# Four column groups of an input projection by seven products, in a stage of their own

## The chip, the cores and the metric

The kernel runs on 1 core of one Trainium2 chip. The metric is the device time of one execution in microseconds (us), lower is better. The kernel before takes 2202.64 us, the median of 3 runs (2201.62 to 2202.83).

## The reference, cut to what matters

One transformer block for 512 tokens of width 2048, in float32. Its first matrix product, `h @ w_in`, is 6680 columns wide and feeds two kinds of attention; then come the output projection, two norms and an MLP of width 8192.

```python
h = rms_norm(x, norm_mix_pre)
proj = h @ w_in                                   # [512, 2048] @ [2048, 6680]
q_a, kv_a, gate_a, q_r, k_r, v_r, g_r = split(proj)   # 1024, 1536, 24, 4 x 1024
kv6 = kv_a.reshape(S, 6, 2, 128)                  # six kinds, two groups of heads, 128 wide
k_cmp = compress_kv(kv6[:, 0], ...)               # gelu(blocks of 32 rows @ w1 + b1) @ w2
v_cmp = compress_kv(kv6[:, 1], ...)
o_a = nsa_attention(q_a, k_cmp, v_cmp, kv6[:, 2], kv6[:, 3], kv6[:, 4], kv6[:, 5],
                    sigmoid(gate_a), t5_bias)     # compressed + selected + window, gated sum
o_r = silu(g_r) * retention(rope(q_r), rope(k_r), v_r)   # four heads of 256
x = x + rms_norm(concat(o_a, o_r) @ w_out, norm_mix_post)
u = square(relu(rms_norm(x, norm_mlp_pre) @ w_up))
x = x + rms_norm(u @ w_down, norm_mlp_post)
```

## The kernel before, in words

**Products in three terms.** Every large product splits both operands into a high and a low part (`split`, L141: ScalarE casts the high part, VectorE subtracts it for the low part). `mm3` (L153) issues three matmuls per tile: high x high, high x low, low x high. The normed input lies in SBUF, transposed, as `Hh` and `Hl` (16 tiles of 128 features by 512 tokens each).

**Slabs and blocks.** A `Slab` (L168) is two feature tiles (256 rows) of up to 512 columns of a weight matrix: `fetch` starts its DMA on SP's queue into a ring of three raw buffers (`wr`), `load` splits it into one of three pairs `whi`, `wlo` (pool `wp`). A block of a projection is eight slabs. `feat_major` (L202) yields outputs with features on the partitions: the weights are the stationary operand, 512 tokens move. `tok_major` (L224) yields outputs with tokens on the partitions: the tokens are stationary and the columns move. One step of the block's work is a chunk of six matmuls; a slab has four chunks. `Driver.run` (L273) walks through the slabs, loads two ahead, and after each chunk calls a pump.

**Side work.** `Side` (L67) keeps a list of units, each with a first and a second part, both generators. `step` advances one second part and one first part; a first part may be one unit ahead. Units are the bias table, the two compressors (`compress`, L483), sixteen attention units (`nsa_unit`, L557; for head group g, query tile i and a pair of heads: scores and softmax as the first part, transposes and products with V as the second, called mix) and four retention heads (`ret_unit`, L683). The pump `two` steps after every second chunk, `three` after three of four. `drain` steps without any projection until given units are done. The order of all engines is the order in which the program issues: each engine works through its own list in order.

**The stages.** (1) The input is loaded, normed and transposed; beside it runs `v0`, the values of the selected branch and the gates (L377, `tok_outer`). (2) Thirteen blocks of `w_in` (L767 to L775): `kv0` (the compressors' inputs, 512 columns), K (keys of the two branches, 512), q0 (queries of group 0, 512), v1 (values of the window branch, 256, token-major), then per retention head QK (feature-major) and VG (token-major), with q1 (queries of group 1) after the first head. Their outputs are evicted from PSUM to where attention reads them: `kv_done`, `k_done`, `q_done`, `v_done`. The ready conditions (`after(n)`, L779) and the table of pumps and drains (L792) tie the side work to the blocks. During the last block (VG3) the mixed heads come back from DRAM (`mixd`) into `Hh`, `Hl`. (3) The output projection. (4) The MLP.

**Seven products.** The MLP already multiplies by seven products instead of eight: both operands are cut in two halves each way, and sums of the quarters are multiplied. `Feed` (L891) loads quarters of a weight group in halves into free slots (`load`), adds quarters on VectorE (`ADD`, L956) or, for product 3, by an accumulating DMA on POOL's queue (`late_sum`), splits each half slab on ScalarE (L961) and VectorE (`low`, L938), up to three slabs ahead (`advance`, `slab`). `ORDER` is 0, 2, 1, 4, 3, 5, 6. `Later` runs work some slabs later.

Of the kernel before, what the change touches and what calls it, by code (L numbers as in the profile page):

```python
# [112 lines left out]
def block_kernel(ctx: ExitStack, tc: tile.TileContext, x, norm_mix_pre, w_in, cmp_pe_k, cmp_w1_k, cmp_b1_k,  # L113
# [54 lines left out]
    class Slab:  # L168
# [11 lines left out]
        def load(self):  # L180
# [4 lines left out]
            hi = pool.tile([P, KC, width], F32R, name="whi")  # L185
            lo = pool.tile([P, KC, width], F32R, name="wlo")
# [77 lines left out]

    side = Side()
# [36 lines left out]
    gw.tile([P, 16], F32, name="gap_w")  # L302
    wp = wctx.enter_context(tc.tile_pool(name="wp", bufs=3, side="right"))
    pool_a = lambda: (wp, S)
    actx, rctx = ExitStack(), ExitStack()
    ap = actx.enter_context(tc.tile_pool(name="att", bufs=1))


    def x_load(t, q):
        if q == 0:  # L310
            xts[t] = ap.tile([P, DM], F32, name="xt", tag="P", bufs=2)
# [4 lines left out]
    ones = ap.tile([1, P], F32, name="ones")  # L316
# [4 lines left out]
    g1 = ap.tile([1, DM], F32, name="g1", tag="P", bufs=2)  # L321
# [4 lines left out]
    gb = ap.tile([P, DM], F32, name="gb", tag="big")  # L326
# [15 lines left out]
    def x_square(t, q):  # L342
        if q == 0:
            hx[t] = ap.tile([P, DM if t % 2 else NG * 32 + DM], F32, name="h", tag="qT" if t % 2 else "kT")
            sx[t] = ap.tile([P, 8], F32, name="st", bufs=2)
# [11 lines left out]
    Vh = ap.tile([P, NT, 2, NG * DK], F32R, name="Vh")  # L357
    Vl = ap.tile([P, NT, 2, NG * DK], F32R, name="Vl")
    gat = ap.tile([P, NT, 3 * HA], F32, name="gat")

    def v_done(b):
        def done(t, ps):
# [3 lines left out]
            split(Vh[:, t, b, :], Vl[:, t, b, :], ps[:, :NG * DK])  # L366
# [9 lines left out]
    ep = ectx.enter_context(tc.tile_pool(name="early", bufs=NSLAB))  # L376
    v0 = slabs_of(w_in, [(OFF_KV + 768, NG * DK), (OFF_GATE, 3 * HA)], lambda: (ep, NG * DK + 3 * HA))  # L377
    first = tok_outer(v0, NG * DK + 3 * HA, v_done(0))
    kv0 = slabs_of(w_in, [(OFF_KV, 512)], pool_a)
# [9 lines left out]
    for i in range(3, NSLAB):  # L389
        v0[i].fetch(wp.tile([P, KC, S], F32, name="raw", tag="whi" if i % 2 else "wlo"))  # L390
        if i in (3, 4):
            x_load(1, i - 1)
# [11 lines left out]
    for n in range(4 * NT):  # L404
# [20 lines left out]
        if n == 3:  # L425
            kv0[0].fetch()
            kv0[1].fetch()
        if n in (7, 11):
            kv0[n // 11].load()
# [6 lines left out]
    ectx.close()  # L436
    rp = rctx.enter_context(tc.tile_pool(name="ret", bufs=1, side="right", reuse_waits="tile"))
# [40 lines left out]
    def kv_done(f, ps):  # L478
        if f % 2 == 0:
            KV[f // 2] = ap.tile([P, NG * S + CBLK], F32, name="KV", tag="P", bufs=2)  # L480
        nc.scalar.copy(KV[f // 2][:, f % 2 * S:(f % 2 + 1) * S], ps)

    def compress(i):  # L483
        pe, w1, b1, w2 = ((cmp_pe_k, cmp_w1_k, cmp_b1_k, cmp_w2_k), (cmp_pe_v, cmp_w1_v, cmp_b1_v, cmp_w2_v))[i]
        kv = KV[i]
        pes = ap.tile([CBLK, DK], F32, name="pes")
# [3 lines left out]
        w2s = ap.tile([DK, DK], F32, name="w2s")  # L490
        nc.sync.dma_start(w2s, w2[0])
        w1s = [ap.tile([P, 16, DK], F32, name="w1s", tag=("qT", "big")[c]) for c in range(2)]
        for c in range(2):
            nc.sync.dma_start(w1s[c], w1[0][c * 16 * P:(c + 1) * 16 * P, :].rearrange("(l p) n -> p l n", p=P))
            yield
# [10 lines left out]
        hs = ap.tile([65, DK], F32, name="hs")  # L506
# [5 lines left out]
        z = ap.tile([DK, 4, 63], F32, name="z")  # L512
# [25 lines left out]
    def k_done(f, ps):  # L538
        nc.scalar.copy(kW[:, f % 2, :] if f // 2 else kS[:, f % 2, 32:], ps)

    def q_done(g):
        def done(f, ps):
            if f == 0:
                QT[g] = ap.tile([P, 4, S], F32, name="qT", tag="qT")
            nc.scalar.copy(QT[g][:, f, :], ps)
        return done
# [10 lines left out]
    def nsa_unit(g, i, pr):  # L557
# [7 lines left out]
        def scores():  # L565
# [40 lines left out]
            if g == 0 and i == NT - 1 and pr == 1:  # L606
                load_bias(1)
            nc.vector.tensor_reduce(negm[:, 4:6], Pt[:, 2:4, :L], axis=AX, op=ALU.max, negate=True)
# [938 lines left out]
```

## Time and profile before

| | |
|---|---|
| median of 3 runs | 2202.64 us |
| the profiled execution | 2200.95 us, span 2199.0 us |
| granted TensorE clock, mean | 0.994 |
| instructions in the profile | 31984 |
| DMA | 348.97 MB, 159 GB/s on the mean |
| HBM read, written | 305.14 MB, 41.75 MB |

The page of the profile gives busy times per engine, the chain of work that ended last, and the costliest groups of instructions. A group's row reads: line, engine, operation, tiles written and read, shape, count, then busy time and the mean of one in ns, then the idle time of the engine before them and what ended it. Matmuls overlap in the pipeline, so the duration of one is longer than the distance to the next. In a row of the windows view stand the stretch, then per engine the busy time and the number of instructions, then the granted clock, the share of the DMA engines and GB/s. In a row of the timeline stand start and duration in us, and in brackets the idle time before it with what ended it. PEld is TensorE's weight load.

### The profile page before, as it was taken

The numbers are of one execution on the slowest core, as the hardware profiler recorded it, in microseconds if no ns is written. First come the engines' busy times: TensorE is split into PE (matmuls) and PEld (weight loads), VectorE is DVE, ScalarE is ACT, GpSimd is POOL, SyncE is SP. The second block draws the span as 40 slices with busy tenths as digits, with TensorE's granted clock in tenths as the row PEclk, the third lists the DMA queues.
The fourth block names the chain that finished last, engine by engine and source line by source line (L and its number), as shares of the span: only waits on it lengthen the run. The fifth ranks groups of instructions, "written<-read, shape, count | busy, mean of one in ns | idle before, by whom it ended". The sixth has DMA issues, their size and how long they took to land.

```text
span 2199.0 us, 31984 instructions
## 1 busy us (share of the span) xinstructions
PE 2154.7 (98%) x12787; PEld 1910.5 (87%) x12787; DVE 1535.1 (70%) x1828; ACT 984.4 (45%) x1425; POOL 122.7 (6%) x139
## 2 busy tenths in 40 slices
PE   8999999999999999999999999999999999999995
PEld 7888878878788899999999999999888888888874
DVE  6213555554555533578988877777878999999996
ACT  5213343343232323485554555555664454445453
POOL 0000000000000000000000000000000000000011
PEclk9999999999999999999999999999999999999997
DMA  6543324322324334577877757676775757566684
GB/s 198 135 120 90 94 65 96 94 75 82 86 75 124 109 101 129 176 233 214 230 218 205 207 165 204 168 205 184 235 230 166 213 157 224 145 202 185 189 220 99
DMA packets 255462, 348.97 MB, mean 159 GB/s; under 512 B 16299, under 2 KB 166139, under 8 KB 254417
## 3 DMA queue, kind: packets, MB, share of 16 engines
q1 hardware_dynamic: 199472, 263.07, 38.0%
q0 software_dynamic: 29616, 42.96, 11.8%
q10 hardware_dynamic: 26226, 40.91, 5.1%
q8 instruction: 100, 1.64, 0.3%
q14 instruction: 48, 0.39, 0.1%
HBM read 305.14 MB, written 41.75 MB: 158 GB/s over the span
## 4 chain that ended last, share of the span: by engine, by line
PE 90%; DVE 5%; issue 1%; ACT 1%; DMA 1%; POOL 0%; SPq 0%; DVEq 0%; ACTq 0%; POOLq 0%
PE prod L157 17%; PE prod L155 17%; PE prod L156 17%; PE mm L155 11%; PE mm L157 11%; PE mm L156 11%; PE S L584 2%; DVE wlo L938 2%; PE PT L647 1%; PE S L707 1%; PE oT L742 1%; PE oT L502 1%; PE oT L155 1%; PE oT L156 1%; PE oT L157 1%
## 5 line engine op out<-in xcount | busy, mean ns | idle before, releaser
L961 ACT CAST whi<-Y 128x1024 fp32r<-128x1024 f32 x227 | 238.2, 1050 | 283.1 <-PE prod L157 117.6
L156 PE MATMUL prod<-wlo,Hh 128*128 128x512 f32 x896 | 349.4, 390 | 2.3 <-DVE wlo L938 2.1
L157 PE MATMUL prod<-whi,Hl 128*128 128x512 f32 x896 | 348.7, 389 | 0.0
L155 PE MATMUL prod<-whi,Hh 128*128 128x512 f32 x896 | 348.6, 389 | 0.0
L144 DVE TENSOR_TENSOR wlo<-raw,whi 128x1024 fp32r<-128x1024 f32 (+4 forms) x152 | 168.6, 1113 | 255.1 <-ACT whi L143 254.6
L961 ACT CAST whi<-low 128x1024 fp32r<-128x1024 f32 x215 | 226.4, 1054 | 265.1 <-PE prod L157 131.6
L938 DVE TENSOR_TENSOR wlo<-Y,whi 128x1024 fp32r<-128x1024 f32 x227 | 276.8, 1220 | 51.5 <-ACT whi L961 50.5
L938 DVE TENSOR_TENSOR wlo<-low,whi 128x1024 fp32r<-128x1024 f32 x215 | 262.1, 1221 | 55.9 <-ACT whi L961 55.0
L157 PE MATMUL prod<-Hh,wlo 128*128 128x256 f32 x1024 | 284.3, 278 | 5.1 <-DVE wlo L938 5.1
L155 PE MATMUL prod<-Hh,whi 128*128 128x256 f32 x1024 | 284.6, 278 | 0.3 <-ACT Hh L143 0.3
L156 PE MATMUL prod<-Hl,whi 128*128 128x256 f32 x1024 | 284.0, 277 | 0.9 <-DVE Hl L144 0.9
L143 ACT CAST whi<-raw 128x1024 fp32r<-128x1024 f32 (+4 forms) x152 | 145.6, 960 | 302.0 <-PE mm L156 147.9
L155 PE MATMUL mm<-whi,Hh 128*128 128x416 f32 (+4 forms) x704 | 262.3, 373 | 0.6 <-ACT Hh L143 0.5
L157 PE MATMUL mm<-whi,Hl 128*128 128x416 f32 (+4 forms) x704 | 248.1, 352 | 0.7 <-DVE Hl L144 0.7
L156 PE MATMUL mm<-wlo,Hh 128*128 128x416 f32 (+4 forms) x704 | 247.6, 352 | 0.0
L155 PE MATMUL mm<-Hh,whi 128*128 128x512 f32 x512 | 214.7, 419 | 0.1
L155 PE MATMUL prod<-sx,whi 128*128 128x256 f32 x768 | 212.0, 276 | 0.0
L156 PE MATMUL prod<-sx,whi 128*128 128x256 f32 x768 | 212.0, 276 | 0.0
L157 PE MATMUL prod<-sx,wlo 128*128 128x256 f32 x768 | 212.0, 276 | 0.0
L156 PEld LDWEIGHTS prod<-wlo,Hh 128*128 128x128 f32 x896 | 168.2, 188 | 40.1 <-DVE wlo L938 5.3
L157 PE MATMUL mm<-Hh,wlo 128*128 128x512 f32 x512 | 200.5, 392 | 0.0
L156 PE MATMUL mm<-Hl,whi 128*128 128x512 f32 x512 | 200.0, 391 | 0.0
(273 smaller groups left out, 3909.4 us busy)
## 6 DMA issues: line engine op xcount, KB each, us to landing
raw<-in_w_in SPq DMA_DIRECT2D x160, 256.0 KB, 3.1
low<-in_w_up SPq DMA_DIRECT2D x76, 512.0 KB, 4.3
Y<-in_w_up SPq DMA_DIRECT2D x64, 512.0 KB, 4.7
low<-in_w_down SPq DMA_DIRECT2D x64, 512.0 KB, 4.6
Y<-in_w_down SPq DMA_DIRECT2D x64, 512.0 KB, 4.6
Y<-ud SPq DMA_DIRECT2D x49, 512.0 KB, 8.0
ud<-Y ACTq DMA_DIRECT2D x77, 256.0 KB, 4.8
raw<-in_w_out SPq DMA_DIRECT2D x32, 416.0 KB, 3.5
```

Of the source, the lines that this page charges most:

```text
L143: nc.scalar.copy(hi, src)
L144: nc.vector.tensor_sub(lo, src, hi.bitcast(F32))
L155: nc.tensor.matmul(ps, ah, bh, start=first, stop=False, skip_group_check=more)
L156: nc.tensor.matmul(ps, ah, bl, start=False, stop=False, skip_group_check=more)
L157: nc.tensor.matmul(ps, al, bh, start=False, stop=last, skip_group_check=more)
L502: nc.tensor.matmul(hid[:65, :DK], kv[:, l:l + STRIDE * 64 + 1:STRIDE], w1s[l // 16][:, l % 16, :], start=l == 0, stop=l == CBLK - 1)
L584: nc.tensor.matmul(sps[:, :c + L], QT[g][:, h, qs], k, start=True, stop=True)
L647: nc.tensor.transpose(pt[:, e * P:(e + 1) * P], Pt[:, e, rows_of(j)], ident)
L707: nc.tensor.matmul(sps[:, :n], QK[:, 2 + d, rows_of(j)], QK[:, d, j * P:], start=d == 0, stop=d == 1)
L742: nc.tensor.matmul(o[:, :DR], AT[:, a0:a0 + P], vr[:, j, :], start=j == 0, stop=j == i)
L938: nc.vector.tensor_sub(lo, src, hi.bitcast(F32))
L961: nc.scalar.copy(hi, src)
```

## The change

Four groups of 512 columns of `w_in` (compressor inputs, keys, queries of group 0, queries of group 1) leave the list of blocks. They are multiplied by seven products with the MLP's `Feed`, in a stage between the input stage and the other projections. The four sums of quarters of the activations are made on VectorE (`in_sums`), one step after every second chunk, beside v1 and then beside the first groups. The operand sums take 8 tiles `sv`; five half slots and three raw buffers borrowed from `wr` hold weights. Each product goes into one PSUM bank (a quarter of the output: two tiles of 128 features by 256 tokens); `in_done` adds the products to the four output quarters, and ScalarE's queue stores them to DRAM (`pd`). The values (v0 and v1) go through DRAM as well (`vd`), since the attention's pool is now opened after this stage. POOL's queue brings all of it back: `k_load` and `v_load` ahead of the first QK block, `kv_load` as the first compressor starts, `q_load` with the bias of its group.

The v1 block moves to the start. The blocks are now v1, the stage of four groups, then QK and VG of four heads, and the output projection. All attention lies beside QK0 to QK3; the new pump `every` steps after each chunk, in QK0 and QK3, `three` in between. The table of drains is new: before the last slab of QK3 it drains to 23 units, so that all but the last retention head is done. Scratch tiles of the compressors share tags, pools get `reuse_waits="tile"`, `wp`'s tiles are 64 elements longer, and the class `Feed` moves up and takes its pool and offsets as arguments. The MLP's use of it is unchanged.

## The diff, cut to its core

```diff
+    def in_source(n):
+        def source(q):
+            h, c0 = q // 10 - 1, INC[n][q % 10 - 1]
+            return w_in[h * 1024:(h + 1) * 1024, c0:c0 + 256].rearrange("(k p) n -> p k n", p=P)
+        return source
+
+    iearly = [(0, 0), (1, 0), (0, 1), (1, 1), (2, 0), (0, 2), (2, 1)]
+    iphases = [((n, p) if p < 2 else n, p, in_source(n)) for n, p in iearly]
+    iphases += [(n, p, in_source(n)) for n in range(len(INC)) for p in ORDER if (n, p) not in iearly]
...
+    ifeed = Feed(iphases, more, 3, [], wp, in_place)
+    IA = [tuple(H[:, 0:8, 0:256] for H in (Hh, Hl)), tuple(H[:, 8:16, 0:256] for H in (Hh, Hl)),
+          (sv[0], sv[1]), (sv[2], sv[3]), (sv[4], sv[5]), (sv[6], sv[7]),
+          tuple(H[:, 8:16, 256:512] for H in (Hh, Hl))]
...
+        def both(p, make):
+            works = [make(c) for c in range(2)]
+            while next(works[0], "end") != "end":
+                yield
+                next(works[1])
+                yield
+            his = [tuple(H[:, 4 * c:4 * c + 4, :] for H in IA[p]) for c in range(2)]
+            for c in range(2):
+                nc.scalar.copy(his[c][0], vs[c])
+            for c in range(2):
+                sub(his[c][1], vs[c], his[c][0].bitcast(F32))
+                yield
...
+        yield from both(2, lambda c: less(vs[c], part(0, 1, c), part(1, 1, c)))
+        yield from both(4, lambda c: more_of(vs[c], sub, part(0, 0, c)))
+        yield from both(5, lambda c: more_of(vs[c], add, part(1, 0, c)))
+        yield from both(3, lambda c: less(vs[c], part(0, 0, c), part(0, 1, c)))
...
+    def groups():
+        sets = []
+        for i, (g, p, _) in enumerate(iphases):
+            n = g if isinstance(g, int) else g[0]
+            more = p in (1, 6)
+            if more:
+                ps = held_in.pop((n, p))
+            else:
+                ps = mm.tile([P, S], F32, name="mm")
+                if p in (0, 3):
+                    held_in[n, {0: 1, 3: 6}[p]] = ps
+            for s in range(2):
+                hi, lo = ifeed.slab()
+                if s == 0 and sets:
+                    in_done(*sets.pop())
+                ilater.step()
...
+                for f in range(2):
+                    for kk in range(4):
+                        k = 4 * s + kk
+                        o = ps[:, f * 256:(f + 1) * 256]
+                        start, last = k == 0 and not f and not more, k == 7 and f == 1
+                        mm3(o, hi[:, kk, rows_of(f)], lo[:, kk, rows_of(f)], xh[:, k, :], xl[:, k, :], start, last,
+                            more)
+                    yield
+            sets.append((n, p, ps))
...
+    drv.steps += tok_major(v1, 256, v_done(1, lambda: ip.tile([P, SL], F32R, name="vst", tag="da", bufs=3)[:, :S]))
+    work = in_sums()
+    sums = lambda c: next(work, None) if c % 2 else None
+    drv.run(2, pump=sums)
+    drv.run(3, pump=sums)
+    ifeed.load(4)
+    drv.run(len(drv.steps) - 2, pump=sums)
+    raws = [wr.tile([P, KC, S], F32, name="raw").rearrange("p k n -> p (k n)") for _ in range(3)]
+    ifeed.free += raws
+    for _ in range(3):
+        ifeed.advance()
+    drv.run(pump=sums)
+    next_up = slabs_of(w_in, [(OFF_QR, DR), (OFF_KR, DR)], pool_a)
+    for n, _ in enumerate(groups()):
+        if n % 2:
+            next(work, None)
+        if raws and not ifeed.loads and all(any(r is f for f in ifeed.free) for r in raws):
+            for i in range(3):
+                next_up[i].fetch()
+            raws = []
+        if ifeed.at == 2 * len(iphases) and not hasattr(next_up[0], "hi"):
+            next_up[0].load()
...
+    def k_load():
+        nc.gpsimd.dma_start(kS[:, :, 32:], pd[G_K, 0].rearrange("p (g n) -> p g n", g=NG))
+        nc.gpsimd.dma_start(kW, pd[G_K, 1].rearrange("p (g n) -> p g n", g=NG))
...
-    drv.steps += feat_major(kv0, 4, kv_done)
-    proj([(OFF_KV + 512, 256), (OFF_KV + 1024, 256)], k_done)
-    proj([(0, 512)], q_done(0))
-    proj([(OFF_KV + 1280, 256)], v_done(1), tok=True)
     for h in range(HR):
         proj([(OFF_QR + h * DR, DR), (OFF_KR + h * DR, DR)], qk_done(h))
         proj([(OFF_VR + h * DR, DR), (OFF_GR + h * DR, DR)], vg_done(h), tok=True)
-        if h == 0:
-            proj([(512, 512)], q_done(1))
...
+    every = lambda c: side.step()
+    def loads():
+        load_bias(0)
+        q_load(0)
+        for _ in range(6):
+            yield
...
+    side.add(lambda: compress(0), nothing)
+    side.add(lambda: compress(1), nothing)
+    side.add(loads, nothing)
     for u in range(8):
+        if u == 4:
+            side.add(*ret_unit(0), after(2), after(3))
+        side.add(*nsa_unit(0, u // 2, u % 2))
+    side.add(*ret_unit(1), after(4), after(5))
     for u in range(8):
+        if u == 4:
+            side.add(*ret_unit(2), after(6), after(7))
+        side.add(*nsa_unit(1, u // 2, u % 2))
+    side.add(*ret_unit(3), after(8))
+    k_load()
+    v_load()
+    for blocks, units, firsts, pump in ((2, 0, 0, every), (3, 0, 0, three), (4, 8, 9, three), (5, 9, 0, three),
+                                        (6, 13, 14, three), (7, 14, 0, three), (8, 23, 23, every)):
         drv.run(blocks * B - 1, pump=pump)
         side.drain(units, firsts)
         drv.run(blocks * B, pump=pump)
```

More of the change, by code (lines that the diff above doesn't have):

```diff
@@ L184, in load @@
             pool, width = self.pool()
-            hi = pool.tile([P, KC, width], F32R, name="whi")
-            lo = pool.tile([P, KC, width], F32R, name="wlo")
+            if pool is wp:
+                hi, lo = (pool.tile([P, SL + 64], F32R, name=name)[:, :SL].rearrange("p (k n) -> p k n", k=KC)
+                          for name in ("whi", "wlo"))
+            else:
+                hi, lo = (pool.tile([P, KC, width], F32R, name=name) for name in ("whi", "wlo"))
             o = 48 if n <= width - 48 else 0
@@ L265, in block_kernel, with __init__, add, step @@
+    class Later:
+        def __init__(self):
+            self.at, self.todo = 0, []
+        def add(self, slabs, work):
+            self.todo.append((self.at + slabs, work))
+        def step(self):
+            self.at += 1
+            due = [w for n, w in self.todo if n <= self.at]
+            self.todo = [(n, w) for n, w in self.todo if n > self.at]
+            for w in due:
+                w()
     side = Side()
@@ L389, in block_kernel @@
     for i in range(3, NSLAB):
-        v0[i].fetch(wp.tile([P, KC, S], F32, name="raw", tag="whi" if i % 2 else "wlo"))
+        v0[i].fetch(wp.tile([P, SL + 64], F32, name="raw", tag="whi" if i % 2 else "wlo")[:, :SL].rearrange(
+            "p (k n) -> p k n", k=KC))
         if i in (3, 4):
@@ L425, in block_kernel @@
         if n == 3:
[L426 to L427 removed]
+            v1[0].fetch()
+            v1[1].fetch()
+        if n == 8:
+            v1[2].fetch()
         if n in (7, 11):
[L429 removed]
+            v1[n // 11].load()
         next(products, None)
@@ L436, in block_kernel @@
     ectx.close()
+    xctx.close()
+    ip = ictx.enter_context(tc.tile_pool(name="groups", bufs=1, reuse_waits="tile"))
+    ip.tile([P, 32], F32, name="gap_i")
+    sv = [ip.tile([P, 8, 2 * P], F32R, name=f"sv{i}") for i in range(8)]
+    more = [ip.tile([P, SL], F32, name=f"half{i}") for i in range(5)]
+    INC = [(OFF_KV, OFF_KV + 256), (OFF_KV + 512, OFF_KV + 1024), (0, 256), (512, 768)]
+    G_KV, G_K, G_Q0, G_Q1 = range(4)
+    pd = dram.tile([len(INC), 2, P, SL], F32, name="pd")
+    def in_source(n):
[3 more added lines that the diff above has]
+        return source
@@ new lines, in block_kernel @@
+    next_up = slabs_of(w_in, [(OFF_QR, DR), (OFF_KR, DR)], pool_a)
[8 more added lines that the diff above has]
+            next_up[0].load()
+    assert not raws
+    ictx.close()
+    ap = actx.enter_context(tc.tile_pool(name="att", bufs=1, reuse_waits="tile"))
@@ L833, in block_kernel @@
     for s in range(NSLAB):
-        drv.run(12 * B + s + 1, pump=lambda c: side.first() if c % 2 else None)
+        drv.run(8 * B + s + 1, pump=lambda c: side.first() if c % 2 else None)
         if s:
@@ L839, in block_kernel @@
     mx.close()
-    drv.run(14 * B - 1, pump=lambda c: side.second() if c % 2 else None)
+    drv.run(10 * B - 1, pump=lambda c: side.second() if c % 2 else None)
     side.drain()
-    drv.run(16 * B)
+    drv.run(12 * B)
     rctx.close()
@@ L1128, in block_kernel @@
     phases += [(("down", c, nb), p, dn_source(c, nb)) for c in range(NCH) for nb in range(2) for p in ORDER]
-    feed = Feed(phases, [low0, low1], 3, [("down", NCH - 1, nb) for nb in range(2)])
+    feed = Feed(phases, halved(low0) + halved(low1), 3, [("down", NCH - 1, nb) for nb in range(2)], hp,
+                lambda g, p, s: 40 if isinstance(g, int) and p == 6 and s else 0)
     tmp = Ring(*xt, *(xh[:, c:c + 512] for c in range(0, 2048, 512)))
```

325 lines of the change are left out of this document (180 added, 145 removed).

## The prediction

> **What bounds the kernel now.** I read the page first (busy shares, chain, groups), then the windows of the stages that the change touches, then the timeline inside them. From the page:
>
> ```profile
> span 2199.0 us, 31984 instructions
> PE 2154.7 (98%) x12787; PEld 1910.5 (87%) x12787; DVE 1535.1 (70%) x1828; ACT 984.4 (45%) x1425; POOL 122.7 (6%) x139
> PE 90%; DVE 5%; issue 1%; ACT 1%; DMA 1%; POOL 0%; SPq 0%; DVEq 0%; ACTq 0%; POOLq 0%
> ```
>
> TensorE is the limit nearly throughout, and 90% of the chain that ended last is its own work. So a change pays if it takes matmul time away, and loses wherever the in-order PE has to wait for VectorE (DVE) or ScalarE (ACT). The stages, from the windows view (PE, PEld, DVE, ACT, POOL busy with counts, clock, DMA share, GB/s):
>
> ```profile
> 300.00:350.00 50.00, 50.00 (x247) 39.05 (x247) 27.59 (x52) 20.54 (x49) 4.62 (x9) 1.00 0.34 82
> 1050.00:1550.00 500.00, 500.00 (x4404) 500.00 (x4403) 401.41 (x399) 268.00 (x318) 35.63 (x28) 1.00 0.72 199
> 1600.00:2100.00 500.00, 500.00 (x2208) 414.01 (x2207) 455.84 (x394) 244.49 (x240) 31.68 (x27) 1.00 0.64 191
> ```
>
> The first row is attention beside a projection at the density "three" (a side step after three of four chunks): PE never idles, DVE is at 55%. The second is the up projection, already by seven products with 256-wide matmuls: 4404 in 500 us, 0.1135 us each, and no idle PE although DVE is at 80%. The third is the down projection, 512 wide: 2208 in 500 us, 0.2264 us each.
>
> **The products.** What goes and what comes have these forms:
>
> ```profile
> L155 PE MATMUL mm<-Hh,whi 128*128 128x512 f32 x512 | 214.7, 419 | 0.1
> L155 PE MATMUL prod<-Hh,whi 128*128 128x256 f32 x1024 | 284.6, 278 | 0.3 <-ACT Hh L143 0.3
> ```
>
> The first row is eight feature-major blocks of 64; the change removes four of them. With the three terms of a split product that is 4 x 64 x 3 = 768 matmuls of 512, 768 x 0.2264 = 173.9 us. It adds 4 groups x 7 products x 16 x 3 = 1344 of 256, 1344 x 0.1135 = 152.6 us. The gain is 21.3 us (the durations of 419 and 278 ns overlap in the pipeline, so I count by rate). By the skill's numbers it would go the other way: the Trainium skill, "TensorE: Matmul & The Clock Gate", section "Back-to-back issue gap", gives a sustained 81 ns at 128 columns and 131 ns at 512 for a stream of weight loads and matmuls. By that, 1344 at no less than 81 ns, 108.9 us, replace 768 x 131 = 100.6 us, an estimate from that page of a loss of at least 8.3 us. The two windows speak against it.
>
> In steady state the new stage is the up projection's pattern: the same Feed, eight half slots, a sum on DVE for products 2, 4 and 6. I cost its middle at nothing: per 2.72 us slab (24 x 0.1135) DVE has one low half (1.22), 6 of 14 times a sum (1.22), and evictions (about 0.25), 2.0 us together. If that cover fails, a slab costs what DVE exceeds 2.72 us by.
>
> **The start of the stage.** Here I find a hole. Rows by line and shape:
>
> ```profile
> L143 ACT CAST whi<-raw 128x1024 fp32r<-128x1024 f32 x96 | 100.6, 1048 | 203.2 <-PE mm L156 138.6 <-DMA raw<-in_w_in 18.9 <-DVE Hl L144 15.8
> L144 DVE TENSOR_TENSOR wlo<-raw,whi 128x1024 fp32r<-128x1024 f32 x96 | 117.3, 1222 | 168.5 <-ACT whi L143 168.4
> L144 DVE TENSOR_TENSOR Vl<-mm,Vh 128x256 fp32r<-128x256 f32 x8 | 3.1, 417 | 2.5 <-ACT Vh L143 2.5
> ```
>
> Three advance() calls stand before the last two slabs of the v1 block. The wp pool has three buffers, so the third one's ACT cast waits until PE has used v1's last slab. Behind it on ACT stand two casts of the operand sum for product 4 (the 13th pump step falls into slab 6) and v1's evictions; DVE's subtractions wait for those casts. The first group product takes the PSUM bank of v1's token tile 0, the fifth in a ring of four, so PE waits for that eviction: three casts 3 x 1.05, the rest of a subtraction 0.17, another 1.22, the eviction's 0.42, together 5.0 us. Bounds: 0 (ACT gets there otherwise) to 7.0 (the third slab's low half, behind three more sums, is late too).
>
> A wait of that kind has a second price here. The timeline and windows of a DVE wait at the start of the up projection:
>
> ```profile
> 990.11 0.28 PE L156 MATMUL prod<-Hl,whi 128*128 128x256 f32 x1
> 994.21 0.38 PE L157 MATMUL prod<-Hh,wlo 128*128 128x256 f32 x1 [3.82 <-DVE wlo L938]
> ...
> 995.00:1000.00 5.00, 5.00 (x32) 5.00 (x31) 4.48 (x5) 2.89 (x4) 1.28 (x1) 0.66 0.96 197
> 1000.00:1005.00 5.00, 5.00 (x46) 5.00 (x46) 4.03 (x4) 2.03 (x3) 0.00 (x0) 1.00 1.17 261
> ```
>
> After 3.82 us of idleness the clock fell to 0.66 in the next window: 32 matmuls instead of 46, 14 x 0.1135 = 1.6 us. So the hole costs 5.0 + 1.6 = 6.6 us.
>
> **Handover to QK0.** Its first slabs are fetched once the borrowed raw buffers are free, about 5 us before the end:
>
> ```profile
> raw<-in_w_in SPq DMA_DIRECT2D x160, 256.0 KB, 3.1
> raw<-in_w_in SPq DMA_DIRECT2D x24, 512.0 KB, 4.6
> out<-Y ACTq DMA_DIRECT2D x4, 1024.0 KB, 7.2
> rd<-rsb POOLq DMA_DIRECT2D x1, 320.0 KB, 8.2
> ```
>
> 3.1 + 1.05 + 1.22 = 5.4 us to a split slab: I take +1.0 (0 to one slab, 2.7).
>
> **Compress and loads.** Keys and values now come back on POOL's queue, in the order rotations, K (two of 512 KB), V (two of 1 MB), bias write, KV. K and V need only space that products 3 and 4 of the last group leave 11 us before its end, so they run under it. The KV load follows the bias matmuls, some 3.5 us into QK0, and lands at 3.5 + 4.6 = 8.1 us; PE needs it at step 9, 8 chunks x 6 x 0.2264 = 10.9 us in, plus bias work. Stores to DRAM lie on ACT's queue and nobody waits soon. For this and the closer steps in QK0 and QK3 I take +1.0 (0 to 3).
>
> **Attention on fewer chunks.** PE does the same attention, beside 7 blocks instead of 12. At "three" the row of 300 to 350 us shows no stall, so blocks VG0 to QK2 cost nothing. But steps run out. QK0 gives 32, the next five blocks 24 each, QK3 28 before its drain: 180. Stepping Side's two rules through the list by hand (a step advances one mix and one scores part) takes 193: table, compress and loads 35, first scores 5, mixes 4 x (5 + 6 + 7 + 8) = 104, three retention outputs 33, where ten retention score steps outlast the mix beside them 10, and 6 in which one waits for the other. So drain(23, 23) issues 13 steps, the rest of one heaviest mix (i = 3) and all of the next, with no projection between. Before, no drain had a step left. That unit, with cover, on the timeline:
>
> ```profile
> 629.70 0.32 ACT L612 ACTIVATE Pc<-Pc,nst 128x31 f32<-128x31 f32 x1
> 633.05 0.18 ACT L612 ACTIVATION_READ_ACCUMULATOR Pt<-Pt,nst 128x1 f32 x1
> ...
> 637.85 0.18 DVE L616 RECIPROCAL nst<-nst 128x6 f32<-128x6 f32 x1
> 638.28 1.68 DVE L622 TENSOR_SCALAR Pt<-Pt,nst 128x512 f32<-128x512 f32 x4
> ...
> 646.12 0.69 DVE L144 TENSOR_TENSOR pl<-PT,ph 128x512 fp32r<-128x512 f32 x1
> 648.04 0.59 ACT L143 CAST ph<-PT 128x512 fp32r<-128x512 f32 x1 [1.96 <-DVE QK L697]
> ...
> 649.24 0.28 PE L155 MATMUL oT<-ph,Vh 128*128 128x256 f32 x1
> 649.94 0.60 PE L647 MATMUL PT<-misc,Pt 128*128 128x128 f32 x4
> ```
>
> Six output matmuls take 0.70 us, four transposes 0.43 (starts 0.108 apart). Uncovered: the first mix waits for low halves behind the scores' reductions on DVE, about 0.7 twice. Then softmax: the exponentials take 3.5 us on ACT, the last pair ending about 0.6 us after the mix's last product; reciprocal, gates and four scalings take 638.28 + 1.68 - 637.85 = 2.1 us more; PE is idle 2.8. In the second mix each transposed block needs 0.59 + 0.69 us and semaphores before PE may use it, with 1.1 us of PE work between: 1.0 before the first product, then 0.1 to 0.2 a step, and 0.7 at its tail. Sum 1.4 + 2.8 + 1.0 + 0.6 + 0.7 = 6.5 us (4 to 9). For the clock I add half of the 1.6 seen above, 0.8. The same page, section "What's actually happening", has the clock halved after an idle window of about 3.4 us; by that the 2.8 us alone would cost nothing and the sum be 0.8 us lower, while the 3.82 us above agree. Against it, 13 uncovered steps save as many switches between side work and projection:
>
> ```profile
> 462.53 0.47 PE L155 MATMUL mm<-Hh,whi 128*128 128x512 f32 x1
> 462.84 0.39 PE L156 MATMUL mm<-Hl,whi 128*128 128x512 f32 x1
> ```
>
> 0.31 us instead of 0.23 after a switch: 13 x 0.09 = 1.2 us back.
>
> **Sum.** -21.3 + 6.6 + 1.0 + 1.0 + 6.5 + 0.8 - 1.2 = -6.6 us. The profiled execution took 2200.95 us, 1.95 above its span; a like one after should have a span of 2192.4. Against the median, 2202.64 - 6.6 = 2196.0 us.
>
> **Rivals.**
> 1. The holes close: the start costs nothing and the drain its lower bound, 4. -21.3 + 1 + 1 + 4 - 1.2 = -16.5, 2186.1 us. For: DVE at 80% in the up stage causes no idle PE. Against: the ring of wp and the bank are fixed by the code.
> 2. The way through DRAM is late. If POOL cannot load K and V until the last group's final eviction (a clearing of one key column is issued only then), 3 MB, the bias write and KV stand behind each other. At the landings above: 2 x 4.6 + 2 x 7.2 + 8.2 + 4.6 = 36.4 us, and PE's first compress matmul waits about 26. At the best rate of the trace,
>
> ```profile
> 950.00:955.00 5.00, 5.00 (x47) 5.00 (x46) 1.28 (x2) 4.97 (x10) 0.55 (x1) 1.00 1.07 388
> ```
>
> the 7 MB of that time (the compressors' 2 MB and QK0's slabs too) take 18 us, and PE waits 7. In the middle, with the clock's 1.6, about 18: 2214 us, slower. It decides once KV lands over 22 us into QK0 (11 us late, which eats 6.6 and 4.4 more). Against: the writes are to other columns, and before, tile-wise reuse let such loads start early.
> 3. A half-width matmul is not half the price: were it bound by its weight load,
>
> ```profile
> L156 PEld LDWEIGHTS prod<-wlo,Hh 128*128 128x128 f32 x896 | 168.2, 188 | 40.1 <-DVE wlo L938 5.3
> ```
>
> 1344 x 0.188 = 252.7 us, 100 more: 2296 us. The 4404 in 500 us have the same operands and exclude this almost surely; the skill's rule above is its only voice.
>
> **Numbers.** A run of this kernel can tell about 0.2%, 4.4 us, from no change. Forecast 0.60: with its bounds 2188 to 2204, so 0.43 faster, 0.17 within. Rival 1: 0.16, faster. Rival 2: 0.20, of which 0.15 slower and 0.05 within (a shorter wait). Rival 3: 0.02; other late waits: 0.02, slower. Together faster 0.59, same 0.22, slower 0.19. Range 2187 to 2208: it leaves out half of rival 1 and the long waits of rival 2.
>
> **What would show it.** In the profile after: about 152 us of prod-like matmuls at 0.1135 with no idle PE in the middle; one wait of about 5 us at the first group product, released by DVE's eviction of v1, with the granted clock below 1 just behind; no wait on a DMA at L502's matmuls; near the end of QK3 a stretch of 15 to 18 us without projection matmuls, PE idle 4 to 9 of them, ended by DVE or ACT. The prediction is wrong if the group stage runs short of DVE or weights all along, if compress waits for KV, or if the drain holds no uncovered steps.

## The result and the profile after

The changed kernel takes 2231.82 us (median of 4 runs, 2231.22 to 2233.57), the kernel before 2202.37 beside it (2201.62 to 2202.83): ratio 1.0135, interval [1.0118, 1.0153]. It is slower by 29.4 us, and the forecast of 2196.0 was wrong, in the sign too. The profiled execution took 2231.42 us.

The lines of the page after that answer to those shown of before:

```profile
span 2229.7 us, 33408 instructions
...
PE 2152.8 (97%) x13363; PEld 1930.4 (87%) x13363; DVE 1634.3 (73%) x1924; ACT 1014.3 (45%) x1453; POOL 144.6 (6%) x165
...
PE 85%; DVE 7%; DMA 3%; ACT 2%; issue 2%; SPq 0%; POOL 0%; ACTq 0%; DVEq 0%; POOLq 0%
```

TensorE is as busy as before in a longer span (a slow-clocked matmul counts as busy too), and 3% of the chain are now DMA, which were 1%. The page of the profile does not show where. The windows view of after does (PE, PEld, DVE, ACT, POOL busy with counts, clock, DMA share, GB/s). Its rows are the middle of the group stage, the QK0 block, the start of QK3, and QK3's drain.

```profile
90.00:220.00 130.00, 130.00 (x1145) 129.89 (x1144) 103.34 (x97) 56.38 (x61) 11.36 (x10) 1.00 0.72 187
230.50:313.10 82.60, 67.84 (x337) 54.89 (x336) 17.66 (x34) 12.75 (x19) 7.47 (x14) 0.90 0.65 187
...
625.00:660.00 35.00, 29.55 (x123) 22.37 (x122) 25.20 (x50) 10.44 (x28) 2.74 (x5) 0.95 0.22 64
701.70:723.30 21.60, 17.70 (x93) 13.90 (x91) 12.07 (x23) 8.52 (x22) 0.00 (x0) 0.84 0.02 6
```

In the group stage 1145 matmuls of 256 take 130 us, 0.1135 each, without a wait: the gain of the products is there. In QK0 PE is idle for 15 us while DVE is busy 18 of 83 us and ACT 13. The waits view of PE between 60 and 740 us says what ended the waits (total, times, longest):

```profile
PE S L752 <- DVE rsb L753: 8.1, 1, 8.1
PE oT L800 <- ACT KV L796: 6.6, 1, 6.6
PE oT L1047 <- DVE rn L1053: 5.2, 4, 2.7
PE mm L155 <- DVE vst L144: 4.8, 1, 4.8
PE PT L952 <- DVE Pt L927: 2.5, 1, 2.5
PE S L888 <- DVE Pc L879: 2.2, 3, 1.4
PE S L888 <- DVE Pt L889: 1.8, 2, 1.2
PE oT L156 <- DVE pl L144: 1.3, 2, 0.9
PE mm L157 <- DVE wlo L339: 0.4, 1, 0.4
```

That is 32.9 us. The same view of before, between 45 and 705 us, has one line of 0.7 us. To add the clock and the small delays, I sum over the trace by how much the starts of two successive matmuls lie further apart than is usual for their shape (0.1135, 0.2264 and so on). The table has this "lost time" of PE up to 780 us, in us, by place. The columns' bounds are times of each trace; before has its stages at other times, so its row gives the sum alone.

| kernel | start, to 110 | groups | QK0, to 265 | QK0, to 310 | 310 to 600 | 600 to 685 | 685 to 780 | sum |
|---|---|---|---|---|---|---|---|---|
| before | | | | | | | | 11.3 |
| after | 7.5 | 0.6 | 11.5 | 10.0 | 10.2 | 9.9 | 10.1 | 59.8 |
| e1_kv_later | 8.0 | 0.6 | 3.0 | 9.1 | 10.2 | 9.8 | 9.7 | 50.4 |
| e2_sp_free | 7.7 | 0.6 | 12.3 | 1.2 | 10.8 | 8.0 | 9.9 | 50.5 |
| e3_compress_pool | 7.8 | 0.6 | 18.6 | 2.6 | 10.5 | 10.0 | 8.7 | 58.8 |
| e4_every | 8.0 | 0.6 | 11.8 | 9.8 | 20.6 | 5.9 | 10.6 | 67.3 |
| e5_two_advances | 9.5 | 0.5 | 10.9 | 9.0 | 10.4 | 10.1 | 10.0 | 60.4 |
| e6_third_head_late | 7.9 | 1.5 | 11.6 | 9.5 | 11.9 | 4.1 | 0.9 | 47.4 |
| e8_four_repairs | 9.2 | 1.4 | 3.1 | 1.2 | 12.4 | 3.9 | 0.5 | 31.7 |
| e12_all | 3.8 | 1.3 | 3.3 | 1.3 | 12.6 | 3.8 | 0.4 | 26.5 |

Before lost 11.3 us over the same work, after 59.8: 48.5 more, less the 21.3 of the products, is 27.2 us. The level of such sums depends on which distance is called usual; with the median distance of each shape, and from 55 us on, before loses 59.0 and after 105.4, 46.4 more, so a difference between rows is good to about 2 us. The profiled execution is 30.5 us longer; 1.7 of the rest is the clock, at half speed for 6.8 us at the up projection's start where it was 3.4, and about 1.6 us stay unplaced. The gain came, and losses, mostly at five places (the start, two in QK0, two in QK3), ate more than twice as much.

**The chain behind QK0's first wait.** From the timeline of after, ScalarE's splits of QK0's first three slabs:

```profile
226.41 1.05 ACT L143 CAST whi<-raw 128x1024 fp32r<-128x1024 f32 x1 [2.96 <-DVE db L668]
...
231.94 1.04 ACT L143 CAST whi<-raw 128x1024 fp32r<-128x1024 f32 x1 [4.47 <-DVE kT L769]
239.77 1.04 ACT L143 CAST whi<-raw 128x1024 fp32r<-128x1024 f32 x1 [6.79 <-DMA raw<-in_w_in]
```

The third cast waits 6.8 us for its weights. In the order of issue the slab's subtraction stands on DVE ahead of the copy `rsb` of the bias table, and PE's second bias matmul needs the bank that this copy frees. So PE, DVE and ACT all stand, and what all of them wait for is a DMA, two steps behind the engine that PE's row names. The slab's fetch had been issued at 224.7, 15 us before the cast. What else was on its way then, from POOL's timeline and the windows:

```profile
223.01 0.56 POOL L744 DMA_DIRECT2D rot<-in_c_rot  x1 [2.50 <-DVE wlo L339]
223.56 0.73 POOL L840 DMA_DIRECT2D kT<-pd  x1
224.29 0.55 POOL L841 DMA_DIRECT2D kT<-pd  x1
224.83 0.54 POOL L845 DMA_DIRECT2D Vh<-vd  x1
225.35 0.55 POOL L845 DMA_DIRECT2D Vl<-vd  x1
```

```profile
215.00:220.00 5.00, 5.00 (x46) 5.00 (x45) 4.44 (x6) 1.62 (x3) 0.00 (x0) 1.00 0.16 36
...
230.00:235.00 5.00, 4.60 (x20) 2.60 (x19) 2.04 (x4) 1.04 (x1) 0.00 (x0) 1.00 1.05 400
235.00:240.00 5.00, 0.00 (x0) 0.00 (x0) 0.00 (x0) 0.23 (x1) 0.00 (x0) 0.91 1.06 387
240.00:245.00 5.00, 2.29 (x6) 1.58 (x7) 2.09 (x3) 0.81 (x1) 1.09 (x2) 0.50 1.07 308
```

Keys and values, 3 MB, first read by PE at 321 and 341 us, go out together with the slab. The DMA engines run full (1.06) while PE does not issue one matmul in 5 us, and then the clock is at 0.50; from 215 to 220 us the DMA engines were at 0.16.

**The chain behind the second wait.** From the waits of SP's queue (60 to 300 us) and of ACT (225 to 300):

```profile
SPq L786 <- DVE z L813: 16.2, 1, 16.2
```

```profile
ACT whi L143 <- DMA raw<-in_w_in: 20.3, 2, 13.5
```

SP's timeline there:

```profile
271.31 0.35 SPq L786 DMA_DIRECT2D b1s<-in_cmp_b_v  x1
...
277.79 13.41 SPq L176 DMA_DIRECT2D raw<-in_w_in  x8
```

The second compressor's `b1s` has one buffer, so its load waits on SP's queue until the first compressor has used it, 16.2 us. Its other loads and the next weight slabs stand behind it in the same queue, and ACT waits 13.5 us for such a slab (the other of the two waits is the 6.8 above). PE's row names ACT's copy of the compressor (`KV L796`), which only stands behind that cast.

### The profile page after: what moved, and what is told of

Read it like the earlier page. It is cut to its first block, busy times and chain, and to the rows that moved or that the text cites. A ratio compares the mean times of both kernels' runs of the same rounds, so it can differ in the third digit from the quotient of the medians.

```text
span 2229.7 us, 33408 instructions
## 1 busy us (share of the span) xinstructions
PE 2152.8 (97%) x13363; PEld 1930.4 (87%) x13363; DVE 1634.3 (73%) x1924; ACT 1014.3 (45%) x1453; POOL 144.6 (6%) x165
## 4 chain that ended last, share of the span: by engine, by line
PE 85%; DVE 7%; DMA 3%; ACT 2%; issue 2%; SPq 0%; POOL 0%; ACTq 0%; DVEq 0%; POOLq 0%
PE prod L157 16%; PE prod L156 16%; PE prod L155 16%; PE mm L155 10%; PE mm L157 10%; PE mm L156 10%; DVE wlo L339 2%; PE S L888 1%; DMA raw<-in_w_in 1%; PE PT L952 1%; PE S L1012 1%; PE oT L800 1%; PE oT L1047 1%; DMA low<-in_w_up 1%; PE oT L155 1%
## 5 line engine op out<-in xcount | busy, mean ns | idle before, releaser
L144 DVE TENSOR_TENSOR wlo<-raw,whi 128x1024 fp32r<-128x1024 f32 (+4 forms) x120 | 129.3, 1082 | 173.7 <-ACT whi L143 173.1
L143 ACT CAST whi<-raw 128x1024 fp32r<-128x1024 f32 (+4 forms) x120 | 112.0, 936 | 230.5 <-PE mm L157 89.7
L157 PEld LDWEIGHTS prod<-Hh,wlo 128*128 128x128 f32 x1024 | 193.6, 189 | 5.8 <-DVE wlo L339 5.8
L155 PEld LDWEIGHTS prod<-whi,Hh 128*128 128x128 f32 x896 | 168.2, 188 | 35.1
L157 PEld LDWEIGHTS prod<-whi,Hl 128*128 128x128 f32 x896 | 168.2, 188 | 34.6
```

The source lines that it names most:

```text
L143: nc.scalar.copy(hi, src)
L144: nc.vector.tensor_sub(lo, src, hi.bitcast(F32))
L155: nc.tensor.matmul(ps, ah, bh, start=first, stop=False, skip_group_check=more)
L157: nc.tensor.matmul(ps, al, bh, start=False, stop=last, skip_group_check=more)
```

## The experiments

**Taking keys and values away from the slab.**

```diff
-    k_load()
-    v_load()
     for blocks, units, firsts, pump in ...
 def loads():
+    k_load()
     load_bias(0)
     q_load(0)
+    v_load()
```

> The loads of keys and values (3 MB) are issued as the side unit after the compressors starts, keys before the bias loads, values behind the queries, in place of ahead of the QK0 block. Theory (QK0's first wait is its third weight slab, slowed by these loads on the shared DMA engines): the wait of 8.1 us at the second bias-table matmul (PE S L752, ended by DVE rsb) falls below 2 us, the half clock at 239 to 249 us goes with it, the third raw slab lands in under 6 us instead of 15, QK0 gets 9 to 12 us shorter, and the time falls from 2231.8 to 2220 to 2223; a part may come back at the first scores. Rival A (the compressor's inputs, on their way through DRAM, are what is late): QK0 stays within 3 us of its 82.6. Rival B (the density of one step after each chunk makes PE meet VectorE and ScalarE whatever the DMAs do): the wait stays above 5 us.

2223.09 us, ratio to before 1.0098 [1.0083, 1.0113]: 8.7 us faster than after, at the theory's edge. (The kernel before, run beside each batch, took 2201.8 to 2202.9 us, so a difference between runs of two batches is good to about 1 us.) Its wait:

```profile
PE S L752 <- DVE rsb L753: 1.4, 1, 1.4
```

In this kernel's row of the table QK0's first half loses 3.0 instead of 11.5 and nothing else moves by over 1. Taking away shows that these loads are the cause, but not whether by their bytes. A dose was to show that: the values loaded twice.

```diff
     k_load()
     v_load()
+    v_load()
```

> The values are loaded twice ahead of the QK0 block (2 MB more on POOL's queue, the same data); nothing else changes. Theory (the third weight slab shares the DMA engines with the loads of keys and values): the slab lands later by about the time of 2 MB at the 327 to 400 GB/s that the windows show there, 5 to 6 us, and the wait at the second bias-table matmul grows from 8.1 to 12 to 15 us: 2236 to 2239. Rival (a fixed cost of the block's start): the wait stays at 8 us, 2231 to 2233.

2232.41 us [1.0127, 1.0155], and the wait is 8.5 us: no growth. POOL's timeline says why this was no dose:

```profile
236.64 0.53 POOL L845 DMA_DIRECT2D Vh<-vd  x1 [9.88 <-DMA Vh<-vd]
```

The second load, into the same tile, stood on POOL for 9.88 us until the first had landed, and the slab's cast began at 240.96; most of the added bytes came after the slab. So the dose was made smaller instead: keys alone (1 MB), or values alone (2 MB), ahead, the other in `loads`.

```diff
     k_load()
-    v_load()
...
     q_load(0)
+    v_load()
```

That is e13; e14 moves `k_load()` instead, to the place that e1 gives it.

> Only the keys (1 MB) are loaded ahead of QK0, the values (2 MB) behind the queries, after the compressors. Without either ahead the wait at the second bias-table matmul was 1.4 us, with both (3 MB) 8.1. Theory (the third weight slab shares the DMA engines with the bytes that are put ahead of it): the wait lies between, by bytes at 1.4 + 6.7 / 3 = 3.6 us (2.5 to 5), 2223 to 2227 us. Rival (one of the two loads alone holds the slab, or a fixed cost as soon as one is there): under 2 or over 7 us.

> Only the values (2 MB) ahead of QK0, the keys behind the compressors. Theory (bytes): the wait is 1.4 + 2 x 6.7 / 3 = 5.9 us (4.5 to 7), 2225 to 2230 us. Rival (the keys alone hold the slab): under 2 us; (a fixed cost): 8 us.

2225.79 us [1.0089, 1.0120] and 2228.29 [1.0103, 1.0137]. The waits, e13 and e14:

```profile
PE S L752 <- DVE rsb L753: 2.4, 1, 2.4
```

```profile
PE S L752 <- DVE rsb L753: 4.3, 1, 4.3
```

With 0, 1, 2 and 3 MB ahead the wait, each from one profiled execution, is 1.4, 2.4, 4.3 and 8.1 us, and the median time is 2223.1, 2225.8, 2228.3 and 2231.8. The wait rises with each, by more each time, and both middle points lie just under the expected ranges, which took it as proportional. So neither load alone makes the wait, nor a fixed cost; it grows with the bytes that go ahead. The Trainium skill, "DMA: Bandwidth & Descriptors", section "Queues, rings and completion order", says that a DMA engine takes packets in turn from the queues that have work for it. The traces agree in that loads on POOL's queue delay a slab on SP's queue, up to the 8.1 us of wait. Why the third megabyte costs more than the first was not tried.

**The second wait, by its two ingredients.** First, SP's queue without the wait: `b1s` with two buffers and `w2s` in a tile of its own.

```diff
-        b1s = ap.tile([DK, 2], F32, name="b1s")
+        b1s = ap.tile([DK, 2], F32, name="b1s", bufs=2)
-        w2s = ap.tile([P, S], F32, name="w2s", tag="pl", bufs=2)[:DK, :DK]
+        w2s = ap.tile([DK, DK], F32, name="w2s", bufs=2)
```

> b1s gets two buffers and w2s a tile of its own with two buffers, so that SyncE need not stand 16.2 us on b1s of the first compressor before it goes on to w2s, w1s and the next weight slab. Theory (QK0's second wait, 6.6 us at PE oT L800 and what lies around it, is a weight slab queued on SP's queue behind the second compressor's loads): SP still has to wait for the first compressor's w1s, which come free some 4 steps earlier, so most of the wait goes: QK0 4 to 9 us shorter, 2223 to 2228 us. Rival (the compressor's own chain of transpose, copy and matmul, or the density, makes PE wait): no change within 2 us.

2223.75 us [1.0086, 1.0116], 8.1 faster than after; QK0's second half loses 1.2 instead of 10.0. SP still waits for `w1s` (`PE oT L800`, 10.8 us in two waits), but early enough. Second, the same loads on POOL's queue (`nc.gpsimd.dma_start` in place of `nc.sync.dma_start` at all four lines of `compress`).

> All loads of the two compressors (the same bytes) go to POOL's queue in place of SP's, so that no weight slab stands behind them on SP's queue. Theory (the order of SP's queue makes the second wait): the second wait (281 to 289 us) goes, about 9 us with its half clock; the first wait stays, since the 3 MB of keys and values remain, but the compressor's 1 MB starts behind them, so the first compressor may start late: 2222 to 2232 us, with no weight slab waited for after 250 us. Rival (the sharing of the DMA engines alone, not the order): the same bytes move at the same time, and both waits stay, 2230 to 2234. If instead the first compressor waits for its weights behind the keys and values, a new wait ended by a DMA stands at PE oT L800.

2230.73 us [1.0114, 1.0149]. The second wait is gone (2.6 us lost), and the foreseen other one is there, since the first compressor's loads now stand behind the 3 MB. Waits of PE in QK0:

```profile
PE S L752 <- DVE rsb L753: 8.7, 1, 8.7
PE PT L795 <- DMA pes<-in_cmp_pe_k: 3.8, 1, 3.8
PE oT L800 <- DMA w1s<-in_cmp_w_k: 1.7, 1, 1.7
```

The load of `b1s` still waits, now on POOL's queue, and for longer:

```profile
280.43 0.58 POOL L786 DMA_DIRECT2D b1s<-in_cmp_b_v  x1 [21.10 <-DVE z L813]
```

No weight slab stands behind it there, and PE has no wait from 275 to 290 us. So e2 shortens what holds up SP's queue, e3 takes the slabs out from behind it, and in both the second wait goes: it was the order of SP's queue.

**Density and drain.** The prediction counted places for steps and found 13 too few. So: the dense pump beside all blocks.

```diff
-    ... (2, 0, 0, every), (3, 0, 0, three), (4, 8, 9, three), (5, 9, 0, three),
-        (6, 13, 14, three), (7, 14, 0, three), (8, 23, 23, every)
+    ... every in all seven rows
```

> The pump that steps after every chunk is used beside all eight blocks (224 places for about 193 steps), so that no step is left for the drain before QK3's last slab. Theory (the drain costs 9 to 10 us because its steps have no projection beside them, and the density costs only where a retention head's outputs run at it, some 5 to 8 us once, in QK3): the drain's stretch of 21.6 us is gone, the retention outputs of three heads now run at the higher density and give back 3 to 8 us each beyond the one of before: 2222 to 2240. Rival C (the drain alone): 2221 to 2223, no new waits. Rival D (the density costs everywhere): every block VG0 to QK2 gets 4 us longer or more, above 2240.

2240.25 us [1.0162, 1.0193], 8.4 slower than after, and the drain is as long as it was, a stretch of 21.7 us without projection (21.6 in after). The theory's own premise fell. The reason is in the order of units: head 2's outputs are ready only once VG2 is complete, and the four last attention units of group 1 stand behind them in the list. Stepping the two rules through by hand gives 14 steps for the drain in after and in e4 alike; VG1 and VG2 run out of steps that are ready. The density meanwhile costs. Waits of PE after 310 us in e4:

```profile
PE oT L1047 <- DVE rn L1053: 10.0, 8, 1.8
```

In after this line had 5.2 us. If that is so, the head has to stand later in the list:

```diff
     for u in range(8):
-        if u == 4:
+        if u == 7:
             side.add(*ret_unit(2), after(6), after(7))
         side.add(*nsa_unit(1, u // 2, u % 2))
-    ... (3, 0, 0, three), ... (5, 9, 0, three), ... (7, 14, 0, three), (8, 23, 23, every)
+    ... (3, 0, 0, every), ... (5, 9, 0, every), ... (7, 14, 0, every), (8, 23, 23, three)
```

> The retention head 2 goes to the last but one place of group 1's attention units (it stood ahead of the last four), and VG0, VG1 and VG2 step after every chunk, QK3 at the lower density. The same steps, at other places. Theory (the drain in QK3 comes from the ready condition of head 2's outputs, which may run only from QK3 on with four attention units behind them: 42 steps for 32 places, whatever the blocks before do): counted by hand 2 steps are left for the drain in place of 14, the stretch without projection falls from 21.6 to under 5 us, and head 2's outputs run at the density three: the 9 us of the drain and some 5 of the 8 in QK3 go, the denser VG blocks give back 1 to 4: 2218 to 2224. Rival (places are what is short, or the density is what costs): the drain goes, but the stalls of the denser blocks take its place: 2228 to 2234.

2219.01 us [1.0060, 1.0088], 12.8 faster than after. Behind QK0 no stretch of over 4 us without projection is left; 685 to 780 us loses 0.9 instead of 10.1, and 600 to 685 us 4.1 instead of 9.9. The run changes the order and the densities together. That the density alone leaves the drain as it was, e4 shows; how the rest of the gain is shared between order and density was not tried.

**The start.** Two advances instead of three:

```diff
-    for _ in range(3):
+    for _ in range(2):
         ifeed.advance()
```

> Two advance() calls in place of three stand before v1's last two slabs, so that ScalarE is not held by a third cast, which must wait for a pair of wp that PE still uses, when v1's evictions come. Theory (the start hole is this cast and what stands behind it on ScalarE and VectorE): the wait of 4.8 us at the first group product falls below 1.5 us and the half clock at 75 to 79 us goes, 5 to 7 us in all: 2225 to 2227 us. Rival (the sums and evictions alone fill VectorE there, whatever the third cast does): the wait stays above 3 us, or moves to the third slab of the group stage: 2229 to 2232.

2233.76 us [1.0124, 1.0152]: no gain. As in the rival's second form the wait moved: at the first group product it fell from 4.8 to 2.2 us, and 3.6 us came up one slab later, where PE waits for the second slab's low half. ACT's timeline in e5, and DVE's:

```profile
71.81 0.90 ACT L143 CAST vst<-mm 128x256 fp32r<-128x256 f32 x3
77.60 0.37 ACT L143 CAST vst<-mm 128x256 fp32r<-128x256 f32 x1 [4.89 <-DMA vd<-vst]
```

```profile
78.00 0.42 DVE L144 TENSOR_TENSOR vst<-mm,vst 128x256 fp32r<-128x256 f32 x1 [2.45 <-ACT vst L143]
...
79.48 1.22 DVE L339 TENSOR_TENSOR wlo<-half,whi 128x1024 fp32r<-128x1024 f32 x1
```

v1's fourth eviction needs a buffer of a ring of three, so its cast waits on ACT for the store of the first to DRAM. On DVE the eviction's subtraction waits for that cast, and the second slab's low half is queued behind it; PE goes on at 80.75, when it is done. In after the third `advance()` had put this low half ahead of the evictions, which hid this wait. So the buffer was mended as well: two evictions share one buffer.

```diff
+    halves = []
+    def vst():
+        if not halves:
+            two_of = ip.tile([P, SL], F32R, name="vst", tag="da", bufs=3)
+            halves.extend([two_of[:, S:], two_of[:, :S]])
+        return halves.pop()
-    ... v_done(1, lambda: ip.tile([P, SL], F32R, name="vst", tag="da", bufs=3)[:, :S]))
+    ... v_done(1, vst))
```

> Two advances, and two evictions of v1 share one buffer of the ring of three, so that ScalarE's fourth eviction does not wait for the store of the first. Theory (the hole has two parts: a cast too early, and behind it 4.9 us of ScalarE in the fourth eviction, on a store to DRAM, with the third slab's cast queued behind; with two advances alone the second takes the place of the first): both must go for a gain; one wait of about 2.2 us at the first group product remains, without the half clock: 2226 to 2228. Rival (VectorE's sums fill the place): 2230 to 2234.

2228.81 us (2225.38 to 2229.57) [1.0109, 1.0140], 3.0 faster than after and short of the theory's 2226 to 2228; the start loses 4.0 instead of 7.5. The half clock that was to go is still there, behind a wait of 2.1 us. These 2.1 us were put down to two casts of the operand sums; the next run leaves out the sums beside v1's last slab and makes them up later.

```diff
-    drv.run(pump=sums)
+    drv.run(len(drv.steps) - 1, pump=sums)
+    drv.run()
...
-        if n % 2:
+        if n % 2 or n in (6, 10):
             next(work, None)
```

> As the run before it, and no step of the operand sums beside v1's last slab (they follow beside the first groups, two of them denser). Theory: the remaining 2.2 us are two casts of the operand sums ahead of v1's first eviction on ScalarE; without them the first group product waits under 1 us: 2224 to 2226. Rival (the subtractions of the group slabs on VectorE are what is late): the 2.2 us stay, and the shifted sums wait elsewhere: 2227 to 2231.

2229.10 us [1.0112, 1.0140], with runs spread from 2226.2 to 2233.3 and the same wait of 2.1 us. The casts stand beside the slab before the last, so this edit moved other steps than the ones it meant. DVE's timeline of e10 shows what stands directly ahead of the eviction that PE waits for:

```profile
70.28 2.36 DVE L633 TENSOR_TENSOR sv<-db,sv 128x1024 fp32r<-128x1024 f32 x2
72.55 0.75 DVE L144 TENSOR_TENSOR vst<-mm,vst 128x256 fp32r<-128x256 f32 x2
```

These are the subtractions of the operand sums that belong to the two casts; e11 has them in the same place. No run took them away, so that they hold the 2.1 us is not shown.

**Together.** The edits of e1, e2 and e5; then e6 with them; then the start of e11 in place of e5's.

> Keys and values later, the second buffers of b1s and w2s, and two advances, together. Theory (three separate waits, each with its own cause): the gains add: 8.7 and 8.1 as measured alone, and 5 to 7 for the advances: 2231.8 less 22 to 24, 2208 to 2211. Rival (one wait moves when another goes): 2214 to 2220.

> The three repairs with the third head late. Theory (the products' gain of 21.3 us is there, and the four places of waiting hide it): 2208 to 2211 less 8 to 13: 2195 to 2203, level with or faster than the 2202 of before. Rival (attention beside 7 blocks in place of 12 costs more than these places, spread thin): stays above 2207.

> The start repaired, keys and values later, second buffers of b1s and w2s, the third head late. Theory (the four repairs gave 2203.7 with 9 us of lost time left at the start of the group stage): 6 to 8.5 us less, 2195 to 2198, faster than before by 0.2 to 0.35%. Rival (the lost time at the start moves on): 2201 to 2204.

2217.20 us [1.0052, 1.0079], 2203.73 [0.9998, 1.0016] and 2197.29 [0.9972, 0.9989]. e7 misses its range, and lands in its rival's, by what e5 did not give: 2231.8 - 8.7 - 8.1 + 1.9 = 2216.9. e8 is 13.5 below e7 (e6 alone gave 12.8), just above its range for the same reason; e12 is 6.4 below e8. The gains add, and the last version is faster than before by 0.2%, 5.1 us. Its page and PE's waits between 60 and 720 us:

```profile
span 2194.6 us, 33415 instructions
...
PE 2141.1 (98%) x13363; PEld 1922.4 (88%) x13363; DVE 1633.6 (74%) x1924; ACT 1013.2 (46%) x1453; POOL 144.5 (7%) x165
```

```profile
PE mm L155 <- DVE vst L144: 2.1, 1, 2.1
PE S L897 <- DVE Pt L898: 2.1, 2, 1.1
PE oT L1056 <- DVE rn L1062: 1.9, 2, 1.0
PE S L761 <- DVE rsb L762: 1.4, 1, 1.4
```

By the table it loses 26.5 us to the 11.3 of before, 15.2 more, against 21.3 gained: -6.1, and -5.1 was measured.

## Why the prediction was wrong, step by step

- **The products, -21.3.** Right: 0.1135 us a matmul, and 0.6 us lost in the whole stage. The cover by DVE that was costed at nothing held at 80% (103.3 of 130 us).
- **The start, +6.6.** Right in place and size: a wait of 4.8 us, released by DVE's eviction of v1, the clock at half behind it, 7.5 lost in all. But only half of the mechanism: a second wait, on the buffer of the fourth eviction, lay hidden under the first (e5, e10).
- **Handover, +1.0.** No wait is there; the term was 1.0 too much.
- **Compress and loads and the closer steps in QK0 and QK3, +1.0 (0 to 3). This is the step that failed.** It measures 11.5 + 10.0 in QK0 and 9.9 before QK3's drain. The step asked whether keys, values and KV come in time for those who read them, and they do: no row of PE waits for them. It did not ask what their bytes, and the waits in front of the compressor's loads, do to the weight slabs that use the same DMA engines and the same queue of SP. e1, e13 and e14 show the first, e2 and e3 the second. For QK3 it took over the density "three"'s lack of stalls to a denser pump, where the outputs of a retention head wait for DVE's norm: 3.4 us in two waits. With e6, which puts the head later and at the lower density, these two waits and 5.8 of the 9.9 go.
- **The drain, +6.5 + 0.8 - 1.2.** It is there, with DVE as releaser: 21.6 us of stretch instead of 15 to 18, 10.1 lost instead of 6.1. PE is idle for 3.9 us of the stretch, less than the 4 to 9 of the forecast; the clock's term of 0.8 was too small, since 6.8 us at half clock lie behind the wait, which cost up to 3.4. The count of 13 uncovered steps was near (14), but by luck, for its reason was wrong: places were not short, the steps were not ready (e4, e6). The 2.8 us of idleness before the second mix was 2.5.
- **VG0 to QK2 at nothing.** Nearly: 10.2 us are lost over 290, of which 3.5 are four waits of PE, the longest (1.5 us) at a retention head's outputs. Part of it was lost before too: by the median distances before loses 29.4 us in that stretch of time, after 37.3.
- **Rival 2** gave 2214 for a late way through DRAM. It named the cause (3 MB, and "QK0's slabs too") but let the compressor's first matmul be the one to wait, and made it depend on POOL's loads being issued late. They were issued in time, and that was the harm: early loads that nobody needed yet shared the DMA engines with a slab that was needed at once.

The range's upper end, 2208, left out most of rival 2 and had no case with two such waits.

## What to carry to other kernels

When a change adds transfers, ask not only whether they arrive in time but which transfer that is needed sooner they share the engines or a queue with, and put a load that is needed late behind the weights; here the place of two loads and the buffers of two small tiles were worth 17 us. When steps are left over for a drain, look at which ready condition held them before adding places: more places cost 8 us here, and another order with other densities gained 13. And a gain of 1% in products is seen in the time only once the waits at its edges are repaired one by one; when e5 removed part of one wait, a second that had been hidden took its place.

## What the runs showed of the hardware

The same wait does not always cost the same clock. In e10 and in e12 PE waits 2.1 us at the first group product. Windows of 3.4 us, two of e10 and then two of e12:

```profile
69.80:73.20 3.40, 1.30 (x11) 1.10 (x11) 3.40 (x5) 3.40 (x7) 0.00 (x0) 1.00 0.52 156
73.20:76.60 3.40, 3.40 (x17) 3.40 (x18) 3.40 (x6) 0.01 (x1) 2.86 (x4) 0.50 0.71 173
```

```profile
69.30:72.70 3.40, 1.74 (x16) 1.54 (x14) 3.40 (x5) 3.40 (x8) 0.00 (x0) 1.00 0.53 153
72.70:76.10 3.40, 2.96 (x25) 2.96 (x26) 3.40 (x7) 0.63 (x1) 2.71 (x4) 1.00 0.75 205
```

In e10 the clock was at half for 3.4 us, 17 matmuls instead of 30; in e12 it stayed at 1.00. But for the one at the kernel's end, half-clock spells in all these traces last 3.4, 6.8 or 10.2 us, and the wait of 4.8 us had 3.4 behind it in after and 6.8 in e6 and e13. In each of the 16 traces the spells start on one grid of 3.413 us, which lies elsewhere in each trace: counted from the span's start, at 0.13 us past a multiple of 3.413 in after, at 1.49 in e10, at 1.02 in e12. The windows above are stretches of this grid, to within 0.05 us. In e10 the whole wait falls into one stretch, so PE is busy for 1.30 of 3.40 us, and the clock falls; in e12 the wait lies over two, and PE is busy for 1.74 and 2.96. Over all 16 traces, leaving out the first 30 us and the end, 73 such stretches at full clock have PE busy for less than 44%, and half clock follows all 73; of the 76 between 44 and 66% it follows 9; of the 9733 above 66% none.

The Trainium skill, "TensorE: Matmul & The Clock Gate", section "What's actually happening", has the clock follow a free-running window of 3.413 us; the grid of 3.413 us and its place in each trace agree. It also wants a whole idle window of about 3.4 us before the clock falls; here 2.1 us of idleness were enough in e10 and e11, and PE was busy for 38% of the stretch. The drain of after, too, has a wait of 2.5 us with 6.8 us at half behind it:

```profile
710.32 0.38 PE L156 MATMUL oT<-pl,vch 31*128 31x256 f32 x1 [0.94 <-DVE pl L144]
...
713.28 2.43 PE L952 MATMUL PT<-misc,Pt 128*128 128x128 f32 x8 [2.47 <-DVE Pt L927]
```

Eight transposes behind it take 2.43 us. So waits of 2 to 3 us carry a possible second price of up to 3.4 us, the half of 6.8, depending on where the grid lies. That single runs of one kernel differ by this is not shown, since each kernel has one trace; it fits that of e12's eleven runs the three with a mean clock of 0.994 have spans of 2193.8 to 2194.6 us and the three with 0.992 have 2196.8 to 2198.4.
